# Seven products in every second pair of a down projection: sums through DRAM, some weight differences prepared early

## The chip, the core and the metric

One Trainium2 chip, one core. The metric is the time of one execution in device microseconds (us). The kernel before has a median of 1666.56 us over three runs.

## The reference, cut to what matters

One hybrid decoder layer in float32: `x` is 256 tokens by 2048 channels. A token mixer (two attention branches, a gated merge, an output projection, LayerNorm) gives `x1`. Then, and this is what the change touches:

```python
def conv_gated_mlp(x, w_gate, w_up, conv_w, conv_b, w_down):
    g = causal_dwconv(x @ w_gate, conv_w, conv_b)     # width 3, D_FF = 5632
    h = jax.nn.gelu(g) * (x @ w_up)
    return h @ w_down                                 # 5632 -> 2048
...
x = layer_norm(ALPHA * x + ffn, ln2_g[i], ln2_b[i])
x = x + jax.nn.sigmoid(x @ w_ple_gate[i]) * (p[i] @ w_ple_proj[i])
```

## The kernel before

**Number format.** A float32 value is split into `hi` (rounded to float32r) and `lo` (the rest). A product of two such values is three TensorE passes, hi·hi, hi·lo and lo·hi, summed in PSUM. ScalarE makes `hi` by a copy (line 110), VectorE makes `lo` by a subtraction.

**Units.** All weights come as units of 128 x 2048 floats (1 MiB) in the order of use. `unit()` hands the next one to TensorE and calls `prep()` until two units beyond it are prepared: SP loads two raw tiles of 128 x 1024 (five raw buffers), ScalarE and VectorE write `hi` and `lo` tiles (six buffers each, two of each for a plain unit). SP follows program order. The order on the other engines comes from a planner with a cost model and priorities, except where a block fixes TensorE's order.

**The MLP.** 44 column blocks `n`, each a gate unit (`psg`) and an up unit (`psu`) of 32 matmuls. VectorE and ScalarE combine the banks, run the conv taps and the GELU, and multiply. GpSimd clears two columns of `gp` and copies two more. The product goes as hi and lo into a quarter of a tile `hC` (lines 1269 to 1276).

**The down projection.** It contracts 22 pairs of 128-row blocks, into 2 halves (`nh`) of 1024 columns. A half has four banks C[t][c]: token half t, 512-column block c. A unit of the weight is one pair in one half, hence a 2 x 2 grid of 128 x 512 weight blocks, and the activation is a 2 x 2 grid of 128 x 128 blocks. A classic pair takes eight block products of three passes, 24 matmuls of 512 columns (`dn<-hi,hC`). In the pairs of `DN_S` a Strassen-like scheme (`s_half`, `strassen`) takes seven, 21 matmuls. It needs four sums of activation blocks (`s_sums`, `sums`, tile `hS`) and four differences of weight blocks, which `prep_s` makes with four VectorE subtractions in place on the raw tiles (line 152) before it splits them: four hi and four lo buffers a unit. Extra banks `p1`, `p5`, `p6`, `p7` (`dn_p`) collect shared products over the half; after the last seven-product pair, `fold()` adds them into the residual z (lines 774 and 775) with one ScalarE copy and eight VectorE operations. Then `ev` adds the C banks to z.

Before, `DN_S` has eight pairs, in an order written out by hand so that the two kinds alternate. A pair in `DN_S` keeps only `hS` (seven cells), a classic one only `hC`. Four pairs (`DN_Y`) hold their products in one tile until the end of the MLP, where the sums are made.

In the second half the last two pairs are a tail: their matmuls are ordered by bank, and `end2` starts LayerNorm 2 on each bank as it ends. Then follow the per-layer embedding's two projections (`pp`, then `pg`).

**Large places.** A pool `big` has 15 places of 8 KiB a partition (tag `S8`), handed out as they come free: `x1T` takes four during the MLP, `z1` two and the LayerNorm gains (`lnb`) two until GpSimd has stored `x1d`; `hC`, `hS`, `z2`, the second gains, `pw` and `x2T` follow. One more `hC` lies in the pool `late`.

Of the kernel before, what the change touches and what calls it, by code (L numbers as in the profile page):

```python
# [9 lines left out]
F32 = mybir.dt.float32  # L10
F32R = mybir.dt.float32r
# [3 lines left out]
ALU = mybir.AluOpType  # L15
# [4 lines left out]
P = 128  # L20
D = 2048
S = 256
DFF = 5632
NF = DFF // P
# [28 lines left out]
WO_C = (0, 2, 4, 6, 7)  # L53


DN_S = (1, 4, 6, 9, 11, 14, 16, 19)
DN_Y = (11, 14, 16, 19)
DN_C = tuple(n for n in range(NF // 2) if n not in DN_S)
DN_ORDER = ((0, 1, 2, 4, 3, 6, 5, 9, 7, 8, 11, 10, 14, 12, 16, 13, 19, 15, 17, 18, 20, 21),
            (0, 1, 2, 4, 3, 6, 5, 9, 7, 11, 8, 14, 10, 16, 12, 19, 13, 15, 17, 18, 20, 21))  # L60
AFF1 = ((0, 2, 3), (0, 2))
AFF2 = ((0, 2), (0, 2))
LN_ORDER = (1, 0, 3, 2)
# [7 lines left out]
def tile_block(ctx: ExitStack, tc: tile.TileContext, wu, wfv, wpp, xT_in, x_in, pT_in, wlr,  # L71
               chan, gnorm, lng, ident_in, mask_in, cmask_in, out):
    nc = tc.nc
# [13 lines left out]
    sm = ctx.enter_context(tc.tile_pool(name="sm", bufs=2))  # L87
# [12 lines left out]
    def t2(name):  # L100
        return sm.tile([P, 512], F32, tag="t2", bufs=6, name=name)
# [7 lines left out]
    def copy(o, i, scale=1.0):  # L109
        return nc.scalar.activation(o, i, AF.Copy, bias=0.0, scale=scale)  # L110
# [14 lines left out]
    dn0 = NU - 16 - NF  # L125
# [3 lines left out]
               for nh in range(2) for i, n in enumerate(order[nh]) if n in sset[nh]}  # L129
    ready = {}  # L130

    def lo_tile(u, name):
        o = 0 if any(u in r for r in UA) else LO_SHIFT
        return rlo.tile([P, 1152], F32R, tag="lo", name=f"lo{name}")[:, o:o + 1024]

    def prep_s(u):


        r0, r1 = [ring.tile([P, 1024], F32, tag="raw", bufs=5, name=f"raw{u}_{h}")
                  for h in range(2)]  # L140
        for h, r in enumerate((r0, r1)):
            nc.sync.dma_start(r, wu[u, :, h * 1024:(h + 1) * 1024])
        b12, b11, b22, b21 = r0[:, 0:512], r0[:, 512:1024], r1[:, 0:512], r1[:, 512:1024]

        def split(src, name, e=slice(0, 1024)):
            hi = rhi.tile([P, 1024], F32R, tag="hi", name=f"hi{u}_{name}")[:, e]
            lo = lo_tile(u, f"{u}_{name}")[:, e]
            copy(hi, src)
            nc.vector.tensor_tensor(lo, src, hi.bitcast(F32), ALU.subtract)  # L149
            return [(hi[:, o:o + 512], lo[:, o:o + 512]) for o in range(0, src.shape[1], 512)]  # L150

        sub = lambda o, a, b: nc.vector.tensor_tensor(o, a, b, ALU.subtract)  # L152
        x11, = split(b11, "b11", slice(512, 1024))
        x22, x21 = split(r1, "b2")
        sub(b11, b12, b11)
        sub(b12, b12, b22)
        t3, t1_ = split(r0, "t13")
        sub(b22, b22, b11)
        sub(b21, b21, b22)
        t2_, t4 = split(r1, "t24")  # L160
        ready[u] = [x11, x21, x22, t1_, t3, t2_, t4]

    def prep(pinned=False):
# [130 lines left out]
    def pull(n, gens=mixers):  # L294
        for _ in range(n):
            while gens:
                try:
                    next(gens[0])
                    break
                except StopIteration:  # L300
                    gens.pop(0)
# [92 lines left out]
    for u in range(8):  # L394
        hi, lo = fvu[u]
        for j in range(2):
            kt = 2 * u + j
            a = xT[kt // 4][:, kt % 4, :]
# [6 lines left out]
            for t, i, c in seq:  # L405
                o, n = fch[c]
                w, x = prods[t][i]
# [34 lines left out]
    for t in range(2):  # L442
        for c, (o, n) in enumerate(fch):
            n = min(n, 1024 - o)
# [147 lines left out]
    for n in range(16):  # L592
        h, j = n // 2, n % 2
# [7 lines left out]
        dst = fqk[h // 2][:, h % 2, j]  # L601
        y = t1("fy")
# [97 lines left out]
    def cell(o, i):  # L700

        return o[:, i, 0:P], o[:, i, P:256]

    def s_sums(y):

        a11, a21, a12, a22 = [y[:, k, t * P:t * P + P] for k in range(2) for t in range(2)]
        v = t2("sums").rearrange("p (i t) -> p i t", t=P)
        for i, a, b, op in ((0, a21, a22, ALU.add), (2, a21, a11, ALU.subtract),
                            (1, v[:, 0], a11, ALU.subtract), (3, a12, v[:, 1], ALU.subtract)):
            nc.vector.tensor_tensor(v[:, i], a, b, op)  # L710
        return v

    def sums(y, name, scale=1.0, full=False):


        v = s_sums(y)
        o = s8([P, 8 if full else 7, 256], F32R, name=name)
        parts = [(slice(0, 1), y[:, 0:1, 0:P]),
                 (slice(1, 3), y[:, 1, :].rearrange("p (t n) -> p t n", t=2)),
                 (slice(3, 7), v)] + [(slice(7, 8), y[:, 0:1, P:256])] * full  # L720
        for e, src in parts:
            copy(o[:, e, 0:P], src, scale)
            hi = o[:, e, 0:P].bitcast(F32)
            if scale == 1.0:
                nc.vector.tensor_tensor(o[:, e, P:256], src, hi, ALU.subtract)
            else:
                nc.vector.scalar_tensor_tensor(o[:, e, P:256], src, scale, hi, ALU.mult,
                                               ALU.subtract)
        return o
# [233 lines left out]
    late = ctx.enter_context(tc.tile_pool(name="late", bufs=1))  # L963
# [4 lines left out]
    for n in range(16):  # L968
# [6 lines left out]
        j = n % 2  # L975
# [246 lines left out]

    tc.keep_in_program_order(nc.scalar.preload_act_table_set("gelu_apprx_tanh_and_others"))
    late.tile([P, GAPS[2]], F32, name="gap2")
    hC, hS, hY, yps = {}, {}, [], {}

    def gate_up(name):
        if first:
# [6 lines left out]
    for n in range(NF):  # L1235
        psg = gate_up(f"psg{n}")


        g = t2(f"gp{n}")
        nc.gpsimd.memset(g[:, 0:2], 0.0)  # L1240
        comb(psg, g[:, 2:258])
        cw = [chn[:, c_cw + j * NF + n:c_cw + j * NF + n + 1] for j in range(3)]
        for i in range(2):
            nc.gpsimd.tensor_copy(g[:, 258 + i:259 + i], g[:, 129 - i:130 - i])
        y = t1("yc")
        nc.vector.tensor_scalar(y, g[:, 2:258], cw[2], chn[:, c_cb + n:c_cb + n + 1],
                                ALU.mult, ALU.add)
        y3 = y.rearrange("p (b n) -> p b n", b=2)
        for j, o in ((1, 1), (0, 0)):
            tap = g[:, o:o + 264 - 4 * o].rearrange("p (b n) -> p b n", b=2)[:, :, 0:P]  # L1250
            nc.vector.scalar_tensor_tensor(y3, tap, cw[j], y3, ALU.mult, ALU.add)
        nc.scalar.activation(y, y, AF.Gelu_apprx_tanh, bias=0.0, scale=1.0)
        psu = gate_up(f"psu{n}")
        u = t1("up")
        comb(psu, u)
        pair, j = n // 2, n % 2
        if pair in DN_S:
            if j == 0:
                if pair in DN_Y:
                    if not hY:  # L1260
                        hY.append(s8([P, len(DN_Y), 2, 256], name="hY"))
                    yps[pair] = hY[0][:, DN_Y.index(pair)]
                else:
                    yps[pair] = t2("yp").rearrange("p (k t) -> p k t", t=S)
            nc.vector.tensor_tensor(yps[pair][:, j, :], y, u, ALU.mult)
            if j == 1 and pair not in DN_Y:
                hS[pair] = sums(yps.pop(pair), f"hS{pair}")
        else:
            nc.vector.tensor_tensor(y, y, u, ALU.mult)
            i = DN_C.index(pair)  # L1270
            if i % 2 == 0 and j == 0:
                hC[i // 2] = (s8 if i < 12 else late.tile)([P, 4, 512], F32R,
                                                           name=f"hC{i // 2}")
            dst = hC[i // 2][:, i % 2 * 2 + j, :]
            copy(dst[:, 0:256], y)
            nc.vector.tensor_tensor(dst[:, 256:512], y, dst[:, 0:256].bitcast(F32),
                                    ALU.subtract)
        if n >= 4:
            pull(1)

    for pair in DN_Y:
        hS[pair] = sums(yps.pop(pair), f"hS{pair}")


    z2 = [None, None]
# [15 lines left out]

    def down(nh, tail, mid):
        def cl(pair, j, t):
            i = DN_C.index(pair)
            a = hC[i // 2][:, i % 2 * 2 + j, :]
            return a[:, t * P:t * P + P], a[:, 256 + t * P:256 + t * P + P]

        def ev(t, c, ps):
            g = 2 * nh + c
            with tc.high_priority(P_STAT if tail else 0):  # L1310
                nc.vector.tensor_tensor(z2of(t, g), z2of(t, g), ps, ALU.add)
                if tail:
                    bn(t, g)

        s_half("dn", nh, DN_ORDER[nh], DN_S, cl, lambda pair, i: cell(hS[pair], i), z2of, ev,
               tail, mid, end2, 1 if tail else 3)

    turns = []
# [206 lines left out]
```

## Time and profile before

| | |
|---|---|
| Median of three runs | 1666.56 us (1666.31 to 1667.71) |
| The profiled execution, its own time | 1666.29 us |
| Its span | 1664.5 us |
| Granted TensorE clock | 1.0 |
| Busy: TensorE, VectorE, ScalarE, GpSimd | 1658.4, 1264.9, 884.0, 43.1 us |
| Moved by DMA | 331.04 MB, 199 GB/s in the mean |

The profile follows one execution. Line numbers are those of the functions above. A row of a group gives engine, operation, output and inputs by tile name, count, busy time and mean duration; what stands after the second bar is the engine's idle time just before and what ended it. The chain of work goes back from the last instruction to whatever released each step. "Landing" is the time from the issue of a transfer to its end.

### The profile page before, as it was taken

To read this page: it belongs to the slowest core of one execution; us is meant where nothing else is said; L and a number is where in the kernel's file an instruction comes from. 1 tells how busy PE (TensorE), PEld (TensorE's weight loads), DVE (VectorE), ACT (ScalarE), POOL (GpSimd) and SP (SyncE) were. 2 spreads that over 40 slices of the span, in tenths; PEclk is the share of its full clock that TensorE was granted. 3 is DMA by queue.
4 is the path that set the end of the run, shared out by engine and by line. 5 is a ranking of instruction groups with operands and counts; after the bars stand their busy time and mean duration, and the time that the engine had idled before them with its cause. 6 is when DMAs were issued, how large, how long until landed. Compare 5 with 4: busy or idle time off the path is not lost.

```text
span 1664.5 us, 24153 instructions
## 1 busy us (share of the span) xinstructions
PE 1658.4 (100%) x8966; PEld 1440.9 (87%) x8966; DVE 1264.9 (76%) x1895; ACT 884.0 (53%) x1293; POOL 43.1 (3%) x171
## 2 busy tenths in 40 slices
PE   9999999999999999999999999999999999999998
PEld 8988888888888888888898888888888888888887
DVE  7776877888876757778987777766667798888874
ACT  6755555655554654545475455544444565455543
POOL 0000000000000000000010000000000000000000
PEclk9999999999999999999999999999999999999999
DMA  8755455545664555567655665555555556676554
GB/s 321 248 170 170 169 176 175 185 155 199 202 227 172 172 177 191 190 214 257 229 190 191 215 215 190 190 189 191 190 189 190 177 180 225 215 265 236 175 188 155
DMA packets 92007, 331.04 MB, mean 199 GB/s; under 512 B 10296, under 2 KB 11584, under 8 KB 90736
## 3 DMA queue, kind: packets, MB, share of 16 engines
q1 hardware_dynamic: 91104, 325.29, 57.4%
q0 software_dynamic: 784, 4.20, 0.7%
q8 instruction: 70, 1.15, 0.3%
q14 instruction: 49, 0.40, 0.1%
HBM read 324.20 MB, written 5.25 MB: 198 GB/s over the span
## 4 chain that ended last, share of the span: by engine, by line
PE 98%; DMA 0%; DVE 0%; ACT 0%; POOL 0%; issue 0%; SPq 0%; POOLq 0%
PE dn L753 11%; PE psu L243 9%; PE psg L243 9%; PE psm L243 7%; PE pg L289 5%; PE psu L245 5%; PE psg L245 5%; PE wo L753 4%; PE gv L753 4%; PE psm L245 4%; PE psa L243 4%; PE gr L289 3%; PE dn_p L753 3%; PE fv L408 2%; PE gr L753 2%; PE psa L245 2%
## 5 line engine op out<-in xcount | busy, mean ns | idle before, releaser
L176 DVE TENSOR_TENSOR lo<-raw,hi 128x1024 fp32r<-128x1024 f32 x512 | 623.2, 1222 | 298.1 <-ACT hi L110 296.7
L110 ACT ACTIVATE hi<-raw 128x1024 fp32r<-128x1024 f32 x512 | 540.2, 1059 | 507.3 <-issue 232.9
L243 PE MATMUL psu<-x1T,hi 128*128 128x512 f32 x688 | 240.4, 392 | 0.0
L243 PE MATMUL psg<-x1T,hi 128*128 128x512 f32 x672 | 234.8, 392 | 0.0
L245 PE MATMUL psu<-x1T,lo 128*128 128x256 f32 x688 | 192.3, 280 | 0.0
L245 PE MATMUL psg<-x1T,lo 128*128 128x256 f32 x672 | 187.8, 280 | 0.0
L243 PE MATMUL psm<-xT,hi 128*128 128x512 f32 x512 | 181.2, 396 | 0.0
L243 PEld LDWEIGHTS psu<-x1T,hi 128*128 128x128 f32 x688 | 129.1, 188 | 27.6
L243 PEld LDWEIGHTS psg<-x1T,hi 128*128 128x128 f32 x672 | 126.1, 188 | 27.0
L245 PE MATMUL psm<-xT,lo 128*128 128x256 f32 x512 | 143.2, 280 | 0.0
L245 PEld LDWEIGHTS psu<-x1T,lo 128*128 128x128 f32 x688 | 130.7, 190 | 0.0
L245 PEld LDWEIGHTS psg<-x1T,lo 128*128 128x128 f32 x672 | 127.6, 190 | 0.0
L753 PE MATMUL dn<-hi,hC 128*128 128x512 f32 x448 | 123.8, 389 | 0.0
L243 PEld LDWEIGHTS psm<-xT,hi 128*128 128x128 f32 x512 | 96.2, 188 | 19.7
L110 ACT ACTIVATE hi_t<-raw 128x1024 fp32r<-128x1024 f32 x56 | 59.5, 1062 | 84.4 <-DVE raw L152 69.5
L753 PEld LDWEIGHTS dn<-hi,hC 128*128 128x128 f32 x448 | 84.0, 188 | 17.4
L245 PEld LDWEIGHTS psm<-xT,lo 128*128 128x128 f32 x512 | 97.2, 190 | 0.1
L243 PE MATMUL psa<-oT,hi 128*128 128x512 f32 x256 | 89.5, 392 | 0.0
L149 DVE TENSOR_TENSOR lo_t<-raw,hi_t 128x1024 fp32r<-128x1024 f32 x56 | 68.4, 1222 | 5.2 <-ACT hi_t L110 3.6
L245 PE MATMUL psa<-oT,lo 128*128 128x256 f32 x256 | 71.6, 280 | 0.0
L753 PE MATMUL dn<-lo,hC 128*128 128x512 f32 x224 | 70.2, 389 | 0.0
L289 PE MATMUL pg<-hi,x2T 128*128 128x512 f32 (+1 forms) x256 | 69.7, 380 | 0.0
(375 smaller groups left out, 2992.6 us busy)
## 6 DMA issues: line engine op xcount, KB each, us to landing
raw<-in_wu_dram SPq DMA_DIRECT2D x568, 512.0 KB, 4.0
fvraw<-in_wfv_dram SPq DMA_DIRECT2D x13, 524.0 KB, 7.0
lnb<-in_lng_dram SPq DMA_DIRECT2D x4, 1024.0 KB, 9.5
z<-in_x_dram SPq DMA_DIRECT2D x2, 1024.0 KB, 6.8
praw<-in_wpp_dram SPq DMA_DIRECT2D x4, 512.0 KB, 5.0
x1d<-z POOLq DMA_DIRECT2D x2, 1024.0 KB, 6.2
z<-x1d SPq DMA_DIRECT2D x4, 512.0 KB, 7.5
xraw<-in_xT_dram SPq DMA_DIRECT2D x7, 256.0 KB, 6.9
```

The source lines that it names most:

```text
L110: return nc.scalar.activation(o, i, AF.Copy, bias=0.0, scale=scale)
L149: nc.vector.tensor_tensor(lo, src, hi.bitcast(F32), ALU.subtract)
L176: i = nc.vector.tensor_tensor(lo, raw, hi.bitcast(F32), ALU.subtract)
L243: nc.tensor.matmul(ps, lhsT=hi[i // 8 if hoff == 0 else 0][:, w0 % 1024:w0 % 1024 + P], rhs=a[:, kt % 4, :], start=first and i == 0, stop= ...
L245: nc.tensor.matmul(ps[:, 256:512], lhsT=lo[i // 8 if hoff == 0 else 0][:, w0 % 1024:w0 % 1024 + P], rhs=a[:, kt % 4, 0:256], start=False, ...
L289: nc.tensor.matmul(bs[j][:, 0:m], lhsT=x, rhs=v[:, o:o + m], start=first and i == 0, stop=last and i == 2)
L408: nc.tensor.matmul(fbk[t][c][:, 0:n], lhsT=x, rhs=w[:, o:o + n], start=kt == 0 and i == 0, stop=kt == 15 and i == 2)
L753: nc.tensor.matmul(ps, lhsT=x, rhs=w, start=todo[id(ps)] == total[id(ps)], stop=todo[id(ps)] == 1)
```

## The change

- `DN_S` becomes every second pair, 1, 3, ... 19: ten in each half. The order is the plain one. The host lays the weights out to match.
- Every pair now writes `hC`, also those of `DN_S`: three of their seven activation cells are read there. The four sums are split in the MLP and stored by GpSimd in DRAM (`sd`, 2 x 256 KB a pair); in each half, `prep_s` loads them back on SP into a large place (512 KB).
- For pairs 3, 9, 15 and 19 of both halves (`DN_T`), `park_gen` loads the unit in the MLP (from n = 8 on, one step about every two n), makes the four differences, and GpSimd stores them in DRAM (`td`, 1 MiB). `prep_s` then loads a quarter and a half of the raw unit and the 1 MiB of differences, and subtracts nothing.
- `hY`, `DN_Y` and the sums at the end of the MLP are gone.

```diff
-DN_S = (1, 4, 6, 9, 11, 14, 16, 19)
-DN_Y = (11, 14, 16, 19)
-DN_C = tuple(n for n in range(NF // 2) if n not in DN_S)
-DN_ORDER = ((0, 1, 2, 4, 3, 6, 5, 9, 7, 8, 11, 10, 14, 12, 16, 13, 19, 15, 17, 18, 20, 21),
-            (0, 1, 2, 4, 3, 6, 5, 9, 7, 11, 8, 14, 10, 16, 12, 19, 13, 15, 17, 18, 20, 21))
+DN_ORDER = (tuple(range(NF // 2)),) * 2
+DN_S = (1, 3, 5, 7, 9, 11, 13, 15, 17, 19)
+DN_T = (3, 9, 15, 19)
...
+    parked = {dn0 + nh * (NF // 2) + n: nh * len(DN_T) + i
+              for nh in range(2) for i, n in enumerate(DN_T)}
+    td = dr.tile([len(parked), P, 2048], F32, name="td")
+    sd = dr.tile([len(DN_S), P, 1024], F32, name="sd")
...
+    def park_gen():
+        for u, i in parked.items():
+            w = s8([P, 2048], name=f"td{i}")
+            nc.sync.dma_start(w, wu[u])
+            yield
+            for h in range(2):
+                differences(w[:, 0:1024], w[:, 1024:2048], h)
+            nc.gpsimd.dma_start(td[i], w)
+            yield
...
     def prep_s(u):
...
+        rt = (r0, r1)
+        if u in parked:
+            nc.sync.dma_start(b11, wu[u, :, 512:1024])
+            nc.sync.dma_start(r1, wu[u, :, 1024:2048])
+            w = s8([P, 2048], name=f"td{u}")
+            nc.sync.dma_start(w, td[parked[u]])
+            rt = (w[:, 0:1024], w[:, 1024:2048])
+        else:
+            for h, r in enumerate((r0, r1)):
+                nc.sync.dma_start(r, wu[u, :, h * 1024:(h + 1) * 1024])
+        if dn0 <= u < dn0 + NF:
+            nh, pair = (u - dn0) // (NF // 2), (u - dn0) % (NF // 2)
+            hS[nh, pair] = s8([P, 4, 256], F32R, name=f"hS{nh}_{pair}")
+            nc.sync.dma_start(hS[nh, pair].bitcast(F32), sd[DN_S.index(pair)].rearrange(
+                "p (i n) -> p i n", i=4))
...
         x11, = split(b11, "b11", slice(512, 1024))
         x22, x21 = split(r1, "b2")
-        sub(b11, b12, b11)
-        sub(b12, b12, b22)
-        t3, t1_ = split(r0, "t13")
-        sub(b22, b22, b11)
-        sub(b21, b21, b22)
-        t2_, t4 = split(r1, "t24")
+        if u not in parked:
+            differences(r0, r1, 0)
+        t3, t1_ = split(rt[0], "t13")
+        if u not in parked:
+            differences(r0, r1, 1)
+        t2_, t4 = split(rt[1], "t24")
...
+        if n % 4 == 0:
+            hC[n // 4] = (s8 if n < 40 else late.tile)([P, 4, 512], F32R, name=f"hC{n // 4}")
         if pair in DN_S:
...
+        dst = hC[n // 4][:, n % 4, :]
+        copy(dst[:, 0:256], h)
+        nc.vector.tensor_tensor(dst[:, 256:512], h, dst[:, 0:256].bitcast(F32), ALU.subtract)
+        if pair in DN_S and j == 1:
+            v = s_sums(yp)
+            for i in range(2):
+                w = sm.tile([P, 2, 256], F32R, tag="t2", bufs=6, name="hs")
+                copy(w[:, :, 0:P], v[:, 2 * i:2 * i + 2])
+                nc.vector.tensor_tensor(w[:, :, P:256], v[:, 2 * i:2 * i + 2],
+                                        w[:, :, 0:P].bitcast(F32), ALU.subtract)
+                nc.gpsimd.dma_start(sd[DN_S.index(pair), :, 512 * i:512 * i + 512],
+                                    w.rearrange("p i n -> p (i n)").bitcast(F32))
...
+        steps = 2 * len(parked)
+        if n >= n0 and (n - n0) * steps // (NF - 3 - n0) != (n - n0 + 1) * steps // (NF - 3 - n0):
+            pull(1, parks)
...
+        def st(pair, i):
+            if i < 3:
+                return cl(pair, (0, 1, 1)[i], (0, 0, 1)[i])
+            return cell(hS[nh, pair], i - 3)
```

More of the change, by code (lines that the diff above doesn't have):

```diff
@@ L130, in tile_block @@
     ready = {}
+    parked = {dn0 + nh * (NF // 2) + n: nh * len(DN_T) + i
+              for nh in range(2) for i, n in enumerate(DN_T)}
+    td = dr.tile([len(parked), P, 2048], F32, name="td")
+    sd = dr.tile([len(DN_S), P, 1024], F32, name="sd")
+    hS = {}
     def lo_tile(u, name):
@@ L134, in lo_tile, with differences @@
         return rlo.tile([P, 1152], F32R, tag="lo", name=f"lo{name}")[:, o:o + 1024]
+    def differences(r0, r1, h):
+        b12, b11, b22, b21 = r0[:, 0:512], r0[:, 512:1024], r1[:, 0:512], r1[:, 512:1024]
+        sub = lambda o, a, b: nc.vector.tensor_tensor(o, a, b, ALU.subtract)
+        if h == 0:
+            sub(b11, b12, b11)
+            sub(b12, b12, b22)
+        else:
+            sub(b22, b22, b11)
+            sub(b21, b21, b22)
+    def park_gen():
[7 more added lines that the diff above has]
+            yield
     def prep_s(u):
@@ L140, in prep_s @@
                   for h in range(2)]
-        for h, r in enumerate((r0, r1)):
-            nc.sync.dma_start(r, wu[u, :, h * 1024:(h + 1) * 1024])
         b12, b11, b22, b21 = r0[:, 0:512], r0[:, 512:1024], r1[:, 0:512], r1[:, 512:1024]
+        rt = (r0, r1)
[5 more added lines that the diff above has]
+            rt = (w[:, 0:1024], w[:, 1024:2048])
+        else:
+            for h, r in enumerate((r0, r1)):
[5 more added lines that the diff above has]
+                "p (i n) -> p i n", i=4))
         def split(src, name, e=slice(0, 1024)):
@@ L150, in split @@
             return [(hi[:, o:o + 512], lo[:, o:o + 512]) for o in range(0, src.shape[1], 512)]
-        sub = lambda o, a, b: nc.vector.tensor_tensor(o, a, b, ALU.subtract)
         x11, = split(b11, "b11", slice(512, 1024))
         x22, x21 = split(r1, "b2")
-        sub(b11, b12, b11)
-        sub(b12, b12, b22)
-        t3, t1_ = split(r0, "t13")
-        sub(b22, b22, b11)
-        sub(b21, b21, b22)
-        t2_, t4 = split(r1, "t24")
+        if u not in parked:
[4 more added lines that the diff above has]
+        t2_, t4 = split(rt[1], "t24")
         ready[u] = [x11, x21, x22, t1_, t3, t2_, t4]
@@ L1224, in tile_block @@
     late.tile([P, GAPS[2]], F32, name="gap2")
-    hC, hS, hY, yps = {}, {}, [], {}
+    hC = {}
+    parks = [park_gen()]
+    n0 = 6
     def gate_up(name):
@@ L1256, in tile_block @@
         pair, j = n // 2, n % 2
+        if n % 4 == 0:
+            hC[n // 4] = (s8 if n < 40 else late.tile)([P, 4, 512], F32R, name=f"hC{n // 4}")
         if pair in DN_S:
             if j == 0:
[L1259 to L1264, printed above, removed]
@@ L1265, in tile_block @@
-            nc.vector.tensor_tensor(yps[pair][:, j, :], y, u, ALU.mult)
-            if j == 1 and pair not in DN_Y:
-                hS[pair] = sums(yps.pop(pair), f"hS{pair}")
-        else:
[L1269 to L1277, printed above, removed]
+                yp = t2("yp").rearrange("p (k t) -> p k t", t=S)
@@ new lines, in tile_block @@
+            h = yp[:, j, :]
+        else:
+            h = y
+        nc.vector.tensor_tensor(h, y, u, ALU.mult)
+        dst = hC[n // 4][:, n % 4, :]
[10 more added lines that the diff above has]
+                                    w.rearrange("p i n -> p (i n)").bitcast(F32))
@@ L1278, in tile_block @@
         if n >= 4:
             pull(1)
-    for pair in DN_Y:
-        hS[pair] = sums(yps.pop(pair), f"hS{pair}")
+        steps = 2 * len(parked)
+        if n >= n0 and (n - n0) * steps // (NF - 3 - n0) != (n - n0 + 1) * steps // (NF - 3 - n0):
+            pull(1, parks)
+    while parks:
+        pull(1, parks)
     z2 = [None, None]
@@ L1303, in cl @@
         def cl(pair, j, t):
-            i = DN_C.index(pair)
-            a = hC[i // 2][:, i % 2 * 2 + j, :]
+            a = hC[pair // 2][:, pair % 2 * 2 + j, :]
             return a[:, t * P:t * P + P], a[:, 256 + t * P:256 + t * P + P]
+        def st(pair, i):
+            if i < 3:
+                return cl(pair, (0, 1, 1)[i], (0, 0, 1)[i])
+            return cell(hS[nh, pair], i - 3)
         def ev(t, c, ps):
@@ L1313, in ev @@
                     bn(t, g)
-        s_half("dn", nh, DN_ORDER[nh], DN_S, cl, lambda pair, i: cell(hS[pair], i), z2of, ev,
+        s_half("dn", nh, DN_ORDER[nh], DN_S, cl, st, z2of, ev,
                tail, mid, end2, 1 if tail else 3)
```

## The prediction

> **What bounds the kernel now.** I read the page's busy times first, then the chain of work that ended last, then the same chain in order of time around the down projection.
>
> ```profile
> span 1664.5 us, 24153 instructions
> ...
> PE 1658.4 (100%) x8966; PEld 1440.9 (87%) x8966; DVE 1264.9 (76%) x1895; ACT 884.0 (53%) x1293; POOL 43.1 (3%) x171
> ...
> PE 98%; DMA 0%; DVE 0%; ACT 0%; POOL 0%; issue 0%; SPq 0%; POOLq 0%
> ```
>
> TensorE is busy for 1658.4 of 1664.5 us and carries 98% of the chain. Any saving has to shorten TensorE's own list, and any new cost shows only if TensorE has to wait for it. The profiled execution took 1666.29 us (1.8 us lie around the span); the median of the runs is 1666.56 us, so I work with differences and set them against the median.
>
> The chain in order of time (start, duration, engine, bank and line, number of matmuls):
>
> ```profile
> 781.20 17.00 PE wo L753 x75
> ...
> 798.20 0.68 PE wo_p L753 x3
> ...
> 1333.83 5.49 PE dn L753 x24
> ...
> 1524.96 0.68 PE dn_p L753 x3
> 1525.64 1.36 PE dn L753 x6
> 1527.00 2.04 PE dn_p L753 x9
> 1529.04 33.32 PE dn L753 x147
> 1562.36 1.37 PE pp L289 x6
> ```
>
> The row with 147 matmuls gives 33.32 / 147 = 0.2267 us for each. The down projection runs from 1333.83 to 1562.36, which is 228.53 us. Its count is 2 halves x (14 classic pairs x 24 + 8 seven-product pairs x 21) = 1008, and 1008 x 0.2267 = 228.5 us. So it holds no wait now: nothing but matmuls can be taken out, and every wait the change brings is a new one.
>
> Busy time by stage (gated MLP, first half, second half of the down projection), with DMA share and rate at the end of each row:
>
> ```profile
> 849.83:1333.83 484.00, 484.00 (x2825) 429.24 (x2825) 345.69 (x520) 244.66 (x358) 25.35 (x132) 1.00 0.58 196
> 1333.83:1448.10 114.27, 114.27 (x506) 94.61 (x505) 98.71 (x118) 61.06 (x68) 0.00 (x0) 1.00 0.63 212
> 1448.10:1562.36 114.26, 114.26 (x506) 94.65 (x505) 97.63 (x115) 60.75 (x65) 1.00 (x1) 1.00 0.67 233
> ```
>
> In all three PE is busy for the whole stretch. VectorE is at 71%, 86% and 85%: it is the next engine, and the planner must keep its lo halves ahead of TensorE.
>
> **What the change takes from TensorE.** Ten pairs instead of eight use 21 matmuls instead of 24, in both halves: 2 x 2 x 3 = 12 matmuls, and 12 x 0.2267 = 2.72 us. A half becomes 498 matmuls, 112.9 us. Nothing else on TensorE changes; the two folds stay two. The Trainium skill ("TensorE: Matmul & The Clock Gate", Back-to-back issue gap) gives about 131 ns for a sustained 512-column matmul, by which the saving would be 1.57 us; this trace has 226.7 ns, and the trace decides.
>
> **VectorE and the MLP.** Groups by line (busy us and mean ns before the second bar):
>
> ```profile
> L176 DVE TENSOR_TENSOR lo<-raw,hi 128x1024 fp32r<-128x1024 f32 x512 | 623.2, 1222 | 298.1 <-ACT hi L110 296.7
> L110 ACT ACTIVATE hi<-raw 128x1024 fp32r<-128x1024 f32 x512 | 540.2, 1059 | 507.3 <-issue 232.9
> ...
> L149 DVE TENSOR_TENSOR lo_t<-raw,hi_t 128x1024 fp32r<-128x1024 f32 x56 | 68.4, 1222 | 5.2 <-ACT hi_t L110 3.6
> L149 DVE TENSOR_TENSOR lo_b<-raw,hi_b 128x512 fp32r<-128x512 f32 (+1 forms) x56 | 53.2, 953 | 8.3 <-ACT hi_b L110 8.3
> L152 DVE TENSOR_TENSOR raw<-raw 128x512 f32<-128x512 f32 x56 | 38.7, 691 | 1.6
> L152 DVE TENSOR_TENSOR raw<-raw,raw 128x512 f32<-128x512 f32 x56 | 38.5, 688 | 1.1
> ...
> L710 DVE TENSOR_TENSOR sums<-yp x14: 283/292/293, 646.7 to 1070.7; 128x128 f32<-128x128 f32 x14
> ...
> L725 DVE TENSOR_TENSOR hS<-sums,hS x8: 678/682/685, 895.6 to 1340.4; 128x512 fp32r<-128x512 f32 x8
> ...
> L725 DVE TENSOR_TENSOR hS<-yp,hS x8: 283/350/419, 883.9 to 1072.7; 128x128 fp32r<-128x128 f32 x4, 128x256 fp32r<-128x256 f32 x4
> ...
> L1276 DVE TENSOR_TENSOR hC<-yc,hC 128x256 fp32r<-128x256 f32 x28 | 11.7, 418 | 0.5 <-ACT hC L110 0.5
> ```
>
> A classic unit costs VectorE 2 x 1.222 = 2.44 us. A seven-product unit costs 2 x 0.953 + 2 x 1.222 + 2 x 0.691 + 2 x 0.688 = 7.11 us. With its four differences parked in DRAM it costs 7.11 - 2.76 = 4.35 us. Each half therefore gets 2 x (7.11 - 2.44) = 9.3 us more and 4 x 2.76 = 11.0 us less: 1.7 us less on VectorE, in 112.9 us. The MLP takes the parked work: 8 x 2.76 = 22.1 us, 16 more hC splits of 0.418 (6.7), 20 splits of sums for the stores, which have the same 256 columns a row (8.4), and two more sets of four sums of 0.29 (2.3). It loses eight sets of hS splits, about 0.68 + 0.42 + 0.28 = 1.38 each (11.0), part of which stand after 1333.83 today. Net about +28 us on 345.7 of 484.0, or 71% to 77%. It stays hidden as long as it comes in pieces that the prepared units can absorb. The largest piece of a unit is four differences, four sums and two splits: 2.76 + 1.16 + 0.84 = 4.8 us. Against it stand six hi and six lo buffers, three units of 5.5 us (a unit is 32 matmuls, and 2825 took 484.0). They are full in the MLP:
>
> ```profile
> ACT hi L110 <- PE psu L243: 36.3, 43, 1.7
> ...
> 918.58 0.54 POOL L1220 DMA_DIRECT2D x1d<-z  x1 [8.73 <-DVE z L1084]
> ...
> raw<-in_wu_dram SPq DMA_DIRECT2D x568, 512.0 KB, 4.0
> ...
> lnb<-in_lng_dram SPq DMA_DIRECT2D x4, 1024.0 KB, 9.5
> ...
> praw<-in_wpp_dram SPq DMA_DIRECT2D x4, 512.0 KB, 5.0
> x1d<-z POOLq DMA_DIRECT2D x2, 1024.0 KB, 6.2
> z<-x1d SPq DMA_DIRECT2D x4, 512.0 KB, 7.5
> ```
>
> ScalarE waits for TensorE to give a hi buffer back, 43 times in this group alone, and L176 idles 298.1 us behind it. So the MLP's cost on TensorE is nothing; if the cover were gone, it would be up to those 28 us. GpSimd issues 20 stores of sums and eight of differences. An issue of the same 1024 KB form took 0.54 us and landed after 6.2, so 28 x 0.54 = 15 us are spread over the MLP on an engine that is busy for 25.35 of 484 us there. What is queued behind an issue on GpSimd are the two gp column copies, for which VectorE's conv taps wait; 0.54 us of that is again covered by the prepared units. The new loads on SP (eight of 1024 KB for parking) add, with the stores, 8 + 8 + 5 = 21 MiB: 196 GB/s becomes about 241.
>
> **The down projection's loads.** SP takes loads in program order. A seven-product unit now brings 512 KB of sums, and a parked one 1024 KB of differences on top of 768 KB of raw weight. For the second half that is 22 MiB + 10 x 0.5 + 4 x 0.75 = 30 MiB, with z (2 x 0.5, from x1d), the two gains (lnb, 2 x 1) and the ple weights (praw, 2 x 0.5, and 0.25 of p): 34.25 MiB = 35.9 MB in 112.9 us, 318 GB/s where 233 stand now. The first half has 31 MiB, 32.5 MB, 288 GB/s. What the queue can give:
>
> ```profile
> 12.00:21.00 9.00, 9.00 (x58) 8.70 (x57) 7.56 (x11) 7.61 (x12) 0.00 (x0) 1.00 1.03 412
> ...
> 1405.00:1410.00 5.00, 5.00 (x24) 4.14 (x23) 4.08 (x6) 2.64 (x3) 0.00 (x0) 1.00 0.88 261
> ```
>
> At 1.03 share it moved 412 GB/s for 9 us. In the down projection itself a 5 us stretch gave 261 at 0.88, which is 297 at full share, and the second half's own row gives 233 / 0.67 = 348. I take 348, since it is the same stage and mix over 114 us: 103 of 112.9 us. The ends 297 and 412 stay for the range.
>
> The tightest loop now is raw load to raw load of seven-product units two places apart: the second raw tile's load waits for the first tile of the unit before. It costs 4.0 (landing) + 1.06 (hi) + 1.22 (lo) + 1.38 (two differences) + 1.06 + 1.22 = 9.9 us. TensorE's period for one pair of each kind is 45 x 0.2267 = 10.2 us. Both kernels alternate the two kinds, so this loop is as tight as before, but parked units (pairs 3, 9, 15 and 19) free both raw tiles early and break it. There are then never more than two unparked ones in a row, against four in today's first half and eight in its second, where TensorE never waited. Cost: nothing, unless landing goes well above 4.3 us, since units are also ready a little ahead. The loads of sums and differences can also hold SP, with the next unit's raw loads queued behind, if no large place is free. The end of the MLP frees four (x1T) and parking one; z takes one, and two units ahead need two for sums and one for differences. hC frees as many in the second half as gains, z and ple weights take. Cost: nothing.
>
> **The folds.** A fold's eight VectorE operations follow the last seven-product pair, now pair 19 with two classic pairs behind it. For the first half the output projection shows the same: last such pair, two classic ones and the next half's first. Its 75 matmuls took 17.00 us, 75 x 0.2267, so no wait. For the second half the two classic pairs are the tail, where LayerNorm begins. No row shows a fold there. VectorE in today's tail:
>
> ```profile
> L774 DVE SCALAR_TENSOR_TENSOR z<-z,fold 128x512 f32<-128x512 f32 x12 | 8.2, 686 | 0.0
> ...
> L775 DVE TENSOR_TENSOR fold<-fold,dn_p 128x512 f32<-128x512 f32 x6 | 4.1, 680 | 0.0
> ...
> 1554.24 0.69 DVE L1311 TENSOR_TENSOR z<-z,dn 128x512 f32<-128x512 f32 x1 [4.85 <-PE dn L753]
> 1554.96 0.69 DVE L1300 BATCH_NORM_STATS2 st<-z 128x6 f32<-128x512 f32 x1
> 1556.95 0.69 DVE L1311 TENSOR_TENSOR z<-z,dn 128x512 f32<-128x512 f32 x1 [1.30 <-PE dn L753]
> ...
> 1567.66 2.35 DVE L176 TENSOR_TENSOR lo<-raw,hi 128x1024 fp32r<-128x1024 f32 x2
> ...
> 1569.21 5.56 PE pg L289 x24
> ```
>
> The fold is 4 x 0.685 + 4 x 0.680 = 5.5 us. The tail begins 48 x 0.2267 = 10.88 us before 1562.36, at 1551.48. VectorE is idle up to 1554.24 (four operations fit) and for 1.30 before 1556.95 (two fit). Two are left, 1.4 us, and push the dense stretch behind. That stretch ends in the first two lo halves of the next projection, from 1567.66; the first is done at 1568.9 and is wanted two matmuls after 1569.21, at 1569.7, so 0.8 us are free. Cost 1.4 - 0.8 = 0.6 us; bounds 0 (the planner fits all of it) and 5.5 (it fits none). I take 0.5, near the worked value.
>
> **Sum.** 1666.29 - 2.72 + 0.5 = 1664.07 for a profiled run; on the median 1666.56 - 2.2 = 1664.3 us. A measurement of this kernel tells about 0.2%, 3.33 us, from no change; the whole saving, 2.72 us, is 0.16% and lies inside that.
>
> **Rivals.** *Loads too late* (slower). The second half needs 318 GB/s. At 297, the short stretch's rate, 35.9 MB take 120.9 us, 8.0 more than the matmuls: -2.72 + 8.0 = +5.3, 1671.8 us. It begins to cost below 318 and makes the kernel slower by over 0.2% below 302. For it: late gains (2 MiB) and a parked unit stand together around pairs 8 and 9. Against it: the 348 average and the 412 at the start. The Trainium skill ("DMA: Bandwidth & Descriptors", Where 436 GB/s comes from) puts the HBM side at about 358 GB/s per core; by that the half's loads take 100 us and the rival stays away, though the 412 row shows the figure is no ceiling here. Chance 0.19.
>
> *SP held up by parking* (slower). From n = 36 on, x1T (4) and hC (10) hold 14 of the 15 large places, so a parking load must wait for the store before it, with weight loads behind it on SP. Prepared units cover some 11 us, the store takes 6.2; if the last two loads each cost one unit, 2 x 5.5 - 2.72 = +8.3, 1674.8 us. Chance 0.09.
>
> *The last fold hides nowhere.* -2.72 + 5.5 = +2.8, 1669.3 us, still within 0.2%. Chance 0.07.
>
> *More than the matmuls.* The down projection has no wait to win back, so over 3.33 us can come only with the scatter of the runs (1666.31 to 1667.71) or a shorter end that no row shows: 1663.0 us. Chance 0.11.
>
> My forecast has the remaining 0.54. Faster by over 0.2% is 0.11, within it 0.54 + 0.07 = 0.61, slower 0.19 + 0.09 = 0.28. The range runs from 1663.0 to 1672.0: it takes in the price of late loads and leaves out the held SP queue and the tails of the others.
>
> **What would show it.** Right: 996 matmuls on the dn banks; a down projection of about 225.8 us in unbroken chain pieces (5.44 classic, 4.76 seven-product); an MLP of 484 us with VectorE near 77%; DMA at 280 to 320 GB/s in the two halves. Wrong: rows in the chain that name raw, td or hS loads, or VectorE's lo behind them, inside the down projection (late loads); a long wait of SP before a parking load with ScalarE's hi waiting for raw in the MLP (held SP); a gap before pg's first matmuls above 0.8 us (fold).

## The result, and the profile after

The changed kernel takes 1670.72 us (median of 8 runs, 1669.37 to 1673.41) against 1666.28: ratio 1.0028, 95% interval 1.0017 to 1.0039. It is slower by 4.4 us, although TensorE has 12 matmuls less to do. The profiled execution took 1670.57 us, its span is 1668.8 us.

The page of the changed kernel, and busy time by stage (MLP, first half, and 113.2 us of the second half):

```profile
span 1668.8 us, 24340 instructions
...
PE 1658.7 (99%) x8954; PEld 1438.5 (86%) x8954; DVE 1282.8 (77%) x1939; ACT 891.5 (53%) x1313; POOL 57.8 (3%) x199
...
PE 95%; DMA 2%; DVE 2%; ACT 1%; issue 1%; POOL 0%; SPq 0%; POOLq 0%; ACTq 0%
```

```profile
849.83:1333.89 484.06, 484.06 (x2826) 429.29 (x2825) 370.78 (x584) 247.27 (x374) 40.58 (x162) 1.00 0.70 242
1333.89:1446.82 112.93, 112.93 (x500) 93.47 (x499) 90.83 (x100) 62.53 (x68) 0.00 (x0) 1.00 0.79 289
1446.80:1560.00 113.20, 109.44 (x475) 88.05 (x474) 91.88 (x101) 61.92 (x67) 0.00 (x0) 1.00 0.84 306
```

The MLP (484 us) and the first half (112.93 us, 498 x 0.2267) came out to the tenth as forecast. The loss begins in the second half: of these three stretches it is the only one in which PE is not busy throughout, and in the chain of all, DMA, VectorE and "issue" have shares that were 0% before. From the first matmul of the down projection to the first of `pp`, the changed kernel takes 231.91 us where 996 x 0.2267 = 225.8 would do: 6.1 us lost. By the start times of the matmuls 1.1 us of them lie at pair 11, 2.3 at pair 17 and 2.6 in the tail. (The view shows PE idle for 3.8 us only; around each wait the matmuls also start further apart than 0.2267 us. In the experiments, too, the idle times in the rows of waits are smaller than what the length lost.) About one more follows: from `pg`'s first matmul to the end it takes 96.38 us where the kernel before took 95.53. So -2.7 + 6.1 + 0.9 = +4.3, which is the difference of the spans.

The chain shows where the waits come from (start, duration, what):

```profile
1476.74 5.55 PE dn L790 x25
...
1485.29 13.80 DMA raw<-in_wu_dram
...
1502.12 1.07 ACT hi_t L108
...
1503.22 1.22 DVE lo_t L187
...
1507.95 0.73 PE dn L790 x2
...
1541.14 8.07 DMA raw<-in_wu_dram
...
1549.31 1.07 ACT hi L108
...
1556.89 6.21 PE dn L790 x26
```

Twice it leaves TensorE for a raw tile that was under way: the first tile of pair 11 for 13.80 us, from 1485.29 to 1499.1, and the first of pair 20, in the tail, for 8.07. Behind the former stand ScalarE's hi, VectorE's differences and lo, and TensorE's matmuls of 1507.95. What SP issued then, first in the changed kernel, then in the one before (raw tiles of seven-product units are L169, L170 and L176, before L142; those of classic ones L209, before L172):

```profile
1481.32 0.33 SPq L170 DMA_DIRECT2D raw<-in_wu_dram  x1
1481.70 0.42 SPq L172 DMA_DIRECT2D td<-td  x1
1482.17 0.42 SPq L180 DMA_DIRECT2D hS<-sd  x1
1482.69 1.40 SPq L209 DMA_DIRECT2D raw<-in_wu_dram  x2
1484.14 1.05 SPq L1129 DMA_DIRECT2D lnb<-in_lng_dram  x2
1485.29 0.93 SPq L176 DMA_DIRECT2D raw<-in_wu_dram  x2
1488.41 0.33 SPq L180 DMA_DIRECT2D hS<-sd  x1
```

```profile
1483.62 1.46 SPq L172 DMA_DIRECT2D raw<-in_wu_dram  x2
1485.13 0.92 SPq L1092 DMA_DIRECT2D lnb<-in_lng_dram  x2
1486.59 5.99 SPq L142 DMA_DIRECT2D raw<-in_wu_dram  x2
```

Within 7.4 us the changed kernel issues 0.5 MiB of raw weight, 1 of differences, 0.5 of sums, 1 of raw, the two gains (2), 1 of raw and 0.5 of sums: 6.5 MiB or 6.8 MB. The kernel before issues 4 MiB in 9 us, because its second raw tile of pair 11 has to wait for a buffer (5.99 us for two issues). Its first tile of pair 11, issued at 1486.59, stands directly behind the same gains; it is the slowest raw tile of that stretch, 10.8 us under way, and TensorE did not wait. So the gains alone don't do it: in the changed kernel the differences and sums of the parked pair 9, 1.5 MiB, are queued ahead of them as well, 4.5 MiB ahead of pair 11's first tile (raw 1, gains 2, and these 1.5) instead of 3. The same 15 us in both kernels, before and then after, and the landings of the raw tiles issued around them (1483 to 1503):

```profile
1485.00:1500.00 15.00, 15.00 (x68) 12.43 (x67) 12.15 (x14) 7.72 (x9) 0.00 (x0) 1.00 0.98 368
...
raw<-in_wu_dram SPq DMA_DIRECT2D x7, 512.0 KB, 6.4
...
DMA to landing us min/median/max: 4.9/6.4/10.8
```

```profile
1485.00:1500.00 15.00, 15.00 (x68) 12.43 (x67) 7.04 (x8) 5.83 (x6) 0.00 (x0) 1.00 1.00 401
...
raw<-in_wu_dram SPq DMA_DIRECT2D x7, 512.0 KB, 10.0
...
DMA to landing us min/median/max: 9.0/10.0/14.4
```

The queue is full in both (0.98 and 1.00, 368 and 401 GB/s), but a raw tile takes 10.0 us in the median instead of 6.4, and VectorE is busy for 7.04 us instead of 12.15. Those 5 us it cannot make up in time.

### The profile page after: what moved, and what is told of

It is laid out like the page before. It is cut to its first block, busy times and chain, and to the rows that moved or that the text cites. A ratio compares the mean times of both kernels' runs of the same rounds, so it can differ in the third digit from the quotient of the medians.

```text
span 1668.8 us, 24340 instructions
## 1 busy us (share of the span) xinstructions
PE 1658.7 (99%) x8954; PEld 1438.5 (86%) x8954; DVE 1282.8 (77%) x1939; ACT 891.5 (53%) x1313; POOL 57.8 (3%) x199
## 4 chain that ended last, share of the span: by engine, by line
PE 95%; DMA 2%; DVE 2%; ACT 1%; issue 1%; POOL 0%; SPq 0%; POOLq 0%; ACTq 0%
PE psu L280 9%; PE psg L280 9%; PE dn L790 8%; PE psm L280 7%; PE psu L282 5%; PE psg L282 5%; PE pg L326 5%; PE wo L790 4%; PE gv L790 4%; PE psm L282 4%; PE psa L280 4%; PE dn_p L790 3%; PE gr L326 3%; PE fv L445 2%; PE gr L790 2%; PE psa L282 2%
## 5 line engine op out<-in xcount | busy, mean ns | idle before, releaser
L213 DVE TENSOR_TENSOR lo<-raw,hi 128x1024 fp32r<-128x1024 f32 x504 | 613.3, 1222 | 253.7 <-ACT hi L108 252.4
L108 ACT ACTIVATE hi<-raw 128x1024 fp32r<-128x1024 f32 x504 | 530.4, 1057 | 447.8 <-issue 175.9
L790 PE MATMUL dn<-hi,hC 128*128 128x512 f32 x384 | 108.0, 390 | 0.4 <-ACT hi L108 0.4
L108 ACT ACTIVATE hi_t<-raw 128x1024 fp32r<-128x1024 f32 x48 | 51.0, 1062 | 80.0 <-DVE raw L142 59.9
L790 PEld LDWEIGHTS dn<-hi,hC 128*128 128x128 f32 x384 | 71.9, 188 | 16.1 <-ACT hi L108 1.3
L108 ACT ACTIVATE hi_b<-raw 128x512 fp32r<-128x512 f32 x64 | 53.7, 841 | 43.5 <-DMA raw<-in_wu_dram 21.6
L187 DVE TENSOR_TENSOR lo_b<-raw,hi_b 128x512 fp32r<-128x512 f32 x64 | 60.7, 953 | 13.7 <-ACT hi_b L108 13.6
## 6 DMA issues: line engine op xcount, KB each, us to landing
lnb<-in_lng_dram SPq DMA_DIRECT2D x4, 1024.0 KB, 10.8
```

Source lines behind the costliest of these rows:

```text
L213: i = nc.vector.tensor_tensor(lo, raw, hi.bitcast(F32), ALU.subtract)
L790: nc.tensor.matmul(ps, lhsT=x, rhs=w, start=todo[id(ps)] == total[id(ps)], stop=todo[id(ps)] == 1)
```

## The experiments

Each run has its own runs of the kernel before on the same chip beside it; its medians there were 1666.35 to 1666.65 us. b3 has two executions, the others ten or eleven. "Length" is from the first matmul of the down projection to the first of `pp` in the profiled execution.

| Run | Matmuls less | Median, us | Ratio to before, 95% | Length, us | Without waits |
|---|---|---|---|---|---|
| a1_no_gains | 12 | 1666.26 | 0.9999 (0.9990 to 1.0009) | 227.31 | 225.8 |
| a2_no_gains_ple | 12 | 1666.38 | 0.9999 (0.9990 to 1.0009) | 226.46 | 225.8 |
| a3_no_fold | 12 | 1668.44 | 1.0010 (1.0001 to 1.0020) | 231.16 | 225.8 |
| a4_eight_in_second | 6 | 1666.15 | 0.9998 (0.9989 to 1.0007) | 227.25 | 227.2 |
| b1_gain_pieces | 12 | 1667.32 | 1.0005 (0.9996 to 1.0014) | 228.19 | 225.8 |
| b2_nine | 9 | 1665.20 | 0.9993 (0.9984 to 1.0002) | 227.86 | 226.5 |
| b3_copy_in_first | 12 | 1674.98 | 1.0049 (1.0031 to 1.0068) | 236.58 | 225.8 |
| b4_ten_last_early | 12 | 1667.17 | 1.0003 (0.9994 to 1.0012) | 229.01 | 225.8 |
| c1_nine_late_ple | 9 | 1664.94 | 0.9994 (0.9985 to 1.0003) | 228.19 | 226.5 |
| c2_ten_late_ple | 12 | 1664.69 | 0.9990 (0.9981 to 0.9998) | 227.22 | 225.8 |
| d1_ten_ple_11 | 12 | 1669.39 | 1.0017 (1.0008 to 1.0026) | 230.74 | 225.8 |

**Without the gains' load.**

```diff
+            if li == 1:
+                nc.gpsimd.memset(gb_[i], 1.0 - i)
+            else:
-            nc.sync.dma_start(gb_[i], lng[2 * li + i]...)
+                nc.sync.dma_start(gb_[i], lng[2 * li + i]...)
```

> The changed kernel, with the second LayerNorm's two gain tiles set to 1 and 0 by GpSimd and not loaded: 2 MiB fewer at pair 8 of the second half (the values of gain and bias are left out). Theory A (late loads: transfers that come in bursts queue up in the second half, raw tiles land 8 to 14 us late, VectorE idles and TensorE waits a little later): the 13.8 us landing before pair 11 goes back to 4 to 7 us, the wait at pair 11 (1.1 us) is gone, the ones from the ple loads at pair 14 on (1.2 us at pair 17, 3.6 in the tail, 1.0 after it) stay in part: 1668.0 to 1669.6 us. Rival B (the fold in the tail): no change, 1670.7 +- 1. Rival C (ten alternations in a row are too dense for VectorE whatever the loads): no change or under 0.5 us.

4.5 us less than the changed kernel, more than theory A gave: not only pair 11's wait is gone, but also the later one at pair 17, although the ple loads before it stayed. What is left lies in the tail and behind it (`pg` to the end still takes 96.6 us). What TensorE still waits for, from 1330 to 1575:

```profile
PE dn L790 <- DVE lo L213: 0.8, 1, 0.8
PE pg L326 <- DVE lo L213: 0.4, 1, 0.4
```

**Without gains and ple loads.** The same, with `praw` and `pTr` set by GpSimd in the second half.

> As the run without gains, and the ple weights and p of the second half are set by GpSimd, not loaded: 3.25 MiB fewer in the second half (their values are left out). Theory A: DMA falls from about 300 to 270 GB/s without bursts, as in the first half, which had no wait; all waits inside the half go, 1664 to 1665.5 us. Rival B: the tail's waits of 3.6 and the 1.0 behind them stay, 1668.4 or more. Rival C: waits at seven-product units stay, 1668 or more.

No gain over the first (1666.38 against 1666.26): taking 1.25 MiB more out of the half moved only the wait inside it (226.46 where 225.8 would do). Behind it stand 1 us between `pp` and `pg` and 1.3 from `pg` to the end (96.85 us): what this kernel loses, 3 us, lies all in the tail and after it, where the fold and the parked pair 19 stand. A's forecast of 1664 to 1665.5 was too low. Rival C falls: ten alternations in a row ran in this half without a wait at any seven-product unit.

**Without the second half's fold.**

```diff
         def fold():
+            if nm == "dn" and nh == 1:
+                return
```

> The changed kernel without the second half's fold: one ScalarE copy and eight VectorE operations, 5.5 us, are left out, so the shared products are missing in z. Loads are unchanged. Theory A: the raw tile that lands at the start of the tail, 8 us after its issue, is as late as before, VectorE has nothing else to do and catches up: 1 to 2 us less, 1668.7 to 1669.7. Rival B: the tail's 3.6 us and the 1.0 after it go: 1666.1 to 1667.0. Rival C: at most 1 us.

2.3 us less in the median. By the profiles 0.75 us of that lie in the down projection (231.16 against 231.91) and 1.0 behind it (`pg` to the end takes 95.35 us, not 96.38). The profile understates it: this execution is 0.9 us above its median, and pair 11 lost 2.3 us in it instead of 1.1, ahead of the place of the fold, while the tail lost 0.7 instead of 2.6. The waits at pairs 11 and 17 stay:

```profile
PE dn_p L790 <- ACT hi_t L108: 2.2, 2, 1.2
PE dn L790 <- DVE lo L213: 0.3, 1, 0.3
```

So the fold costs 2 to 3 us (2.3 in the median here; the runs without the gains lost 2.6 and 3.0 in the tail and behind it), and the loads the larger part, the 4.5 us of the run without gains. Both theories have a share, and B is not the main one.

**Eight in the second half.**

```diff
+DN_SS = (DN_S, (1, 3, 5, 7, 11, 13, 15, 17))     # parked in the second half: 3, 15
```

> The first half keeps ten seven-product pairs, the second has eight: pairs 9 and 19 are classic there and neither parked nor loaded with sums, 2.5 MiB fewer in the second half, next to the gains (pair 9) and the tail (pair 19), and the last fold has four classic pairs behind it. TensorE saves 6 matmuls against the kernel before, 1.36 us. Theory A: no wait or under 1 us: 1664.9 to 1665.9. Rival B: the fold is covered as well: the same time, but the wait at pair 11 (1.1) stays, 1666. Rival C: two alternations fewer in a row each: 1665 to 1667.

The length is what its 1002 matmuls need, and `pg` to the end takes 95.57 us as before: no wait at all. This run also tells the gains from the parked pair: the gains still come at once, but pair 9 is not parked, and pair 11's first tile stands directly behind 3 MiB and not 4.5. It landed after 10.4 us, and the raw tiles around it took as long in the median as in the changed kernel, without a wait of TensorE:

```profile
1483.53 1.11 SPq L1130 DMA_DIRECT2D lnb<-in_lng_dram  x2
1485.26 1.47 SPq L177 DMA_DIRECT2D raw<-in_wu_dram  x2
...
DMA to landing us min/median/max: 4.1/10.0/11.9
```

The median, 1666.15, is nearer to before than the profiled run (1665.1); the runs there scattered from 1665.04 to 1670.07, and 1.36 us can't be told from nothing by this interval.

**The same bytes without the burst.** The gains come in eight pieces behind pairs 6 to 13.

```diff
+    def gain_piece(k):
+        ...
+        nc.sync.dma_start(gain[1][k // 4][:, e], lng[2 + k // 4][:, e].broadcast_to([P, 512]))
```

> The changed kernel, all loads kept, but the second LayerNorm's gains come in eight pieces of 256 KB, one behind each of pairs 6 to 13 of the second half, instead of 2 MiB at once behind pair 8. The half loads as many bytes. If the burst was the cause (theory A in its narrow form): the wait around pair 11 goes and the time is near that without gains, 1666 to 1667 us. If it is the half's total (A in its wide form: about 300 GB/s is too much whatever the order): 1669.5 to 1671. Rival C (VectorE): 1670 to 1671.

1667.32: 3.4 us less than the changed kernel, with every byte loaded, 0.3 above the forecast's upper end. The narrow form of theory A holds. What is left is again in the tail and behind it. The queue is as full as before in the same 15 us, but pair 11's tile, which took 13.80 us, now takes 9.31, and VectorE goes on working (11.34 of 15 us):

```profile
1485.00:1500.00 15.00, 15.00 (x68) 12.43 (x67) 11.34 (x12) 7.96 (x8) 0.00 (x0) 1.00 1.00 393
```

```profile
1485.75 9.31 DMA raw<-in_wu_dram
```

**A burst where none was.** SP copies 2 MiB from `td` to an unused place in DRAM behind pair 8 of the first half.

> The changed kernel with a burst put where none was: behind pair 8 of the first half, which had no wait, SP also copies 2 MiB of td to an unused place in DRAM, ahead of the raw loads of pair 11. If bursts are the cause: raw tiles of pair 11 land 8 us later or more, TensorE waits 0.5 to 2 us in the first half, whose length goes from 112.9 to 113.5 or more. If rival C or the total decides: the first half stays at 112.9 (30 MiB and 2 of copy are no more than the second half's).

8.3 us over before, 4.3 over the changed kernel, and more than forecast: the first half takes 4.1 us longer. Pair 11 of the first half now shows what pair 11 of the second did (chain, then landings of loads issued from 1372 to 1390):

```profile
1375.32 14.23 DMA raw<-in_wu_dram
...
1393.69 0.50 PE dn_p L791
...
1456.79 0.68 PE dn_p L791 x3
```

```profile
raw<-in_wu_dram SPq DMA_DIRECT2D x5, 512.0 KB, 13.8
```

The second half's first seven-product pair starts at 1456.79 instead of 1452.26. With the burst the stretch waits, without it not: in the first half of the changed kernel the raw tiles issued from 1372 to 1390 landed after 9.0 us in the median, and nothing waited. Two things came together, though: SP issued pair 11's tiles 2.9 us later than there (1375.32 against 1372.41), and they were under way 3.7 us longer.

Over the runs the time of pair 11's first tile follows what was issued ahead of it and was still under way, not counting a transfer that landed within the next 1 us:

| Where | Ahead, MiB | Landed after, us | TensorE waits at pair 11 |
|---|---|---|---|
| a1, second half | 2.5 | 8.3 | no |
| b1, second half | 3.0 | 9.3 | no |
| a4, second half | 3.0 | 10.4 | no |
| kernel before, second half | 3.0 | 10.8 | no |
| changed kernel, first half | 3.5 | 10.5 | no |
| changed kernel, second half | 4.5 | 13.8 | yes |
| a3, second half | 4.5 | 14.1 | yes |
| b3, first half (2 of them the copies) | 4.5 | 14.2 | yes |

**Nine and ten pairs with the last one earlier.**

```diff
+DN_SS = (DN_S, (1, 3, 5, 7, 9, 11, 13, 15, 17))                # b2: parked 3, 9, 15
+DN_ORDER = (..., tuple(range(16)) + (17, 16, 19, 18, 20, 21))  # b4
```

> Gains in pieces as in the run before, and nine seven-product pairs in the second half: pair 19 is classic there, so four classic pairs stand behind the last one. 9 matmuls fewer than the kernel before, 2.04 us. If bursts and the uncovered fold are all there is: 1664.5 us, no idle TensorE in the down projection, and the next projection starts as before. If the total of the loads decides: 1666 to 1668.

> Gains in pieces, ten seven-product pairs in both halves, but the end of the second half runs in the order 14, 15, 17, 16, 19, 18, 20, 21: three classic pairs behind the last seven-product one, two of which are next to each other (15 and 17). 12 matmuls fewer, 2.72 us. If only bursts and the uncovered fold cost: 1663.8 to 1664.8. If two neighbouring ones are too dense for the six buffers: a wait at pair 17 of 1 to 3 us, 1665 to 1667.

Both stayed above their first case: each keeps one wait next to the ple loads at pair 14, b2 at pair 17 (0.5 us and what follows), b4 at its neighbours 15 and 17 (1.1 us) and one in the tail:

```profile
PE dn_p L791 <- ACT hi_t L109: 0.5, 1, 0.5
```

```profile
PE dn_p L791 <- DVE lo_t L188: 1.1, 1, 1.1
PE dn L791 <- DVE lo L214: 0.8, 1, 0.8
```

In both `pg` to the end is back at 95.4 to 95.6 us: with three or four classic pairs behind the last seven-product one, the fold costs nothing behind the down projection.

**The ple weights later.** Behind the 18th unit (index 17) instead of the 15th; c2 in the order 12, 13, 15, 14, 17, 16, 19, 18, 20, 21.

> Nine seven-product pairs in the second half, gains in pieces, and the ple weights prepared behind pair 17 instead of pair 14, so that their 1.25 MiB, their two raw tiles and their 3 us of VectorE meet classic pairs only. If the ple loads' burst made the wait of 1.2 us at pair 17: no idle TensorE in the down projection, 9 matmuls or 2.04 us saved against the kernel before, 1664.3 to 1664.9 us. If the total of the loads decides: the wait at pair 17 stays, 1665.2 us as without this step. If the tail is now disturbed instead: a wait in the last two pairs, 1665.5 us or more.

> Ten seven-product pairs in both halves, gains in pieces, the ple weights behind the 18th unit, and the second half in the order 12, 13, 15, 14, 17, 16, 19, 18, 20, 21: three classic pairs behind the last seven-product one, and the neighbours are 13 and the parked 15. 12 matmuls fewer, 2.72 us. If bursts and an uncovered fold are all: 1663.8 to 1664.6. If the ple step, now three units before the end, is late itself: a wait of 1 to 3 us in the tail or at pair 19, 1665 to 1667.

c2 is the best version: 1664.69 us, 11 runs within 1664.62 and 1665.22, ratio 0.9990 (0.9981 to 0.9998). It loads the same bytes as the changed kernel, which takes 6 us more; the pieces, the place of the ple step and the order at the end differ together, so this run does not share the 6 us out. In its second half the DMA rate is as high (0.85, 307 GB/s), yet one wait is left, in the tail:

```profile
PE dn L791 <- DVE lo L214: 0.8, 1, 0.8
```

```profile
1446.80:1560.00 113.20, 112.36 (x495) 92.42 (x494) 96.95 (x111) 63.29 (x69) 1.00 (x1) 1.00 0.85 307
```

In c1's profile the wait moved from pair 17 into the tail, as its third case said; but that execution, 1667.76, is the slowest of eleven, and in it the down projection already starts 1.5 us later than in c2's. The median of the others is near 1664.9. c1's gain on b2, 0.3 us, is not told from nothing: the kernel before was 0.3 us faster beside c1 as well.

**The ple weights early, among the pieces.**

> As the last kernel with ten pairs, but the ple weights come behind pair 11 and not three units before the end. It tells what the last wait of that kernel (1.4 us in the tail, on VectorE's lo halves) is: if the ple step next to the fold is its cause, the tail has no wait and the time is 1663.6 to 1664.1 us unless the ple loads, now among the pieces of the gains, hold up pair 13 by 1 us or more (then 1664.7 or above, with the wait there). If the fold and the tail's own units are the cause, the tail's wait stays: 1664.7 us.

4.7 us more than c2: the ple loads now meet the gains' pieces and the parked pair 15, and the waits stand there, while the tail loses 0.3 us:

```profile
PE dn L791 <- ACT hi L108: 1.7, 2, 1.5
PE dn L791 <- DMA hS<-sd: 0.5, 1, 0.5
PE dn_p L791 <- ACT hi_t L108: 0.4, 1, 0.4
```

That fits the ple step beside the fold as the cause of c2's last wait, but does not show it: d1's TensorE comes to the tail some 4 us later, which gives VectorE time to get ahead. A place for the step that costs nothing was not found.

## Why the prediction was wrong, step by step

- **Held:** 12 matmuls and 2.72 us (996 matmuls, every unbroken piece at 0.2267 us); the MLP at 484 us, VectorE 370.78 of 484.06 or 77%, DMA 242 GB/s where 241 stood; SP not held by parking; the first half at 112.9 us with 289 GB/s where 288 stood, its fold covered. GpSimd's 28 stores and 25 us more of VectorE (28 were forecast) cost TensorE nothing.
- **Failed: "The down projection's loads".** I spread 35.9 MB over the whole half, set 103 us of transfers against 112.9 us and took the cost as nothing. The queue did deliver: 401 GB/s where it mattered. But at pairs 9 to 11 some 6.8 MB were asked for within 7.4 us, which needs 17 us at that rate, and most of it stood ahead of pair 11's tiles. The loop was worked out with a landing of 4.0 us, the median of the whole kernel, and called free "unless landing goes well above 4.3 us"; it went to 13.8. The sum should have been made over the stretch of the burst; the rival's text named the gains and a parked unit together, and then let the half's average speak against them. a1 (no gains), a4 (pair 9 not parked) and b1 (the same bytes in pieces) show it: each takes the wait at pair 11 away. The time goes with what is queued at once, not with the bytes of the half.
- **In the same step, "parked units free both raw tiles early and break" the loop:** they do free them. Pair 11's second tile was issued 0.6 us after the first, where the kernel before waited 5.7 us for a buffer. But it was the first tile on which the chain waited, and that stood directly behind the gains in both kernels. What parking added was 1.5 MiB ahead of it, and for that the loop had no term.
- **The rival "loads too late"** named the right thing, loads that come too late, with another reason than the one that the runs show: its +5.3 us are worked out from a queue that gives the half 297 GB/s and no more, while it gave 401 in the burst, and c2's second half has the same loads and takes 114.3 us. That +4.4 us came out near it, and that the time lies in the range, is luck, as 2 to 3 us of the loss are the fold's. What decides is how long one tile is under way: for pair 11's first tile 8.3 to 10.8 us cost nothing, 13.8 to 14.2 brought waits.
- **Mis-sized: the last fold.** I took 0.5 us, bounds 0 and 5.5; without it the kernel was 2.3 us faster in the median, and a2, with neither gains nor ple loads, still lost 3 us in the tail and behind it (beside the parked pair 19, so not all of it need be the fold's). I counted VectorE's idle time in the tail of the kernel before as free. In the changed tail the lo halves of the last two units were late themselves and lay between the fold's operations, and the idle time was spent waiting for the first of them:

```profile
1550.40 1.23 DVE L213 TENSOR_TENSOR lo<-raw,hi 128x1024 fp32r<-128x1024 f32 x1 [1.56 <-ACT hi L108]
1551.54 0.68 DVE L811 SCALAR_TENSOR_TENSOR z<-z,dn_p 128x512 f32<-128x512 f32 x1
1552.14 1.22 DVE L213 TENSOR_TENSOR lo<-raw,hi 128x1024 fp32r<-128x1024 f32 x1
1553.28 0.69 DVE L812 TENSOR_TENSOR fold<-fold,dn_p 128x512 f32<-128x512 f32 x1
1553.87 1.22 DVE L213 TENSOR_TENSOR lo<-raw,hi 128x1024 fp32r<-128x1024 f32 x1
```

- **The bound of 0.2%** put a full success inside "same"; c2's -1.7 us lies there, and its interval just leaves 1 out.

Open: why c2 still waits once in the tail after the ple step, how much of the tail's loss is the fold alone and how much the late lo halves beside it, and what the kernel would do with the gains loaded before the down projection (no large place is free there; it was not tried).

## What to carry to other kernels

When loads are added to a stage that is bound by TensorE, don't compare bytes with the stage's time: lay them out in the order of the queue and look for the stretch where most is issued at once, and what is next behind it. For a transfer that is needed soon, count what is ahead of it when it is issued: here 2.5 to 3.5 MiB of loads cost nothing, and 4.5 made TensorE wait. Two bursts that are each harmless can add up, like the gains and the parked pair. Large loads that are not urgent can be cut into pieces between the urgent ones: here that was worth 3.4 us at no cost in bytes, while 12 matmuls are worth 2.7.

## What the runs showed of the hardware

A load's time is mostly its place in the queue: 512 KB of raw weight landed after 4.0 us in the median of the kernel before, after 8.3 to 10.8 behind 2.5 to 3.5 MiB, and after 13.8 to 14.2 behind 4.5: 2.6 to 3.1 us for each MiB, the tile's own half included. The queue held 384 to 401 GB/s over 15 us in several runs, above the 358 GB/s that the Trainium skill ("DMA: Bandwidth & Descriptors", Where 436 GB/s comes from) gives for one core's share of HBM; here one core ran alone. And prepared units covered landings of up to 10.8 us for pair 11's first tile, but not 13.8, in halves where VectorE is busy for 80 to 85% of the time.
